# Two attentions with normalised inputs: where the norm's factor is multiplied in, and in which layout a norm is taken

## The chip, the cores and the metric

The kernel runs on one core of a Trainium2 chip. The metric is the device time of one execution in microseconds, the median of several runs. The core has five engines with a queue each: TensorE (PE in the profile; PEld is its weight load), VectorE (DVE), ScalarE (ACT), GpSimd (POOL) and SyncE (SP), which here only starts DMAs. Each executes its queue in order.

## What is computed

The reference runs two transformer blocks of two layers each, over 512 tokens (and 16 more in the first block) of width 1024. The change touches only the first layer of the second block, which has two kinds of attention on the same normalised input `hn = rms(h, g)`:

```python
aq, ak, av, bq, bk, bv = split_cols(hn @ w_in, AB_SPLITS)
# attention A, 4 heads: two softmaxes, subtracted
s  = einsum(rope(aq), rope(ak)) * 64**-0.5        # causal; two maps per head
a  = softmax(s)[0] - lam * softmax(s)[1]
ao = a @ av                                       # 128 values per head
ao = rms(ao, g_sub) * (1 - lam_init)              # norm over the 128 values
# attention B, 8 heads, dilated windows
bo = dilated_attention(rope(bq), rope(bk), bv)
y  = concat([ao, bo]) @ w_out
```

`rope(x)` is `x * cos + swap(x) * sin`, where `swap` exchanges the two halves of each head (with the sign in `sin`). Since the norm's factor, one over the root of the mean square, is a number for each token, it can be multiplied to the products of the projection instead of to `h`.

## The kernel before

Data lie transposed: features on the 128 partitions, the 512 tokens along the free dimension. Every fp32 factor is split in a high and a low part, and each product is three matmuls of a reduced fp32 type (`fp32r`): a projection of one 128-column chunk is 24 matmuls of 512 columns (8 chunks of the width, times 3) into one PSUM bank. Weights come by DMA (`wr`), ACT rounds them to `wh`, DVE or POOL takes the rest as `wl`.

The function `mixer_ab` (L1401 on) does the layer's attentions. It works in eight stages, p = 0 to 3 of A (`diff`) and then p = 0 to 3 of B (`dila`), two heads (for A, two maps of a head) in each. A stage makes `v`, then key and query by `qk`: projection, `scaled` (L1429, the PSUM bank times `rstd`, the norm's factor for each token, spread over all partitions), `rope`, and `stack`, which lays the high and low parts of each head (ACT L689, DVE or POOL L690, one DMA) into tiles that the matmuls read. `rope` (L826) is four DMAs of 32 partitions each from `v` into `sw` (L832), POOL's `v * cos` in place (L834), DVE's `sw * sin` (L835) and DVE's sum (L836). After key and query the stage transposes `v` on PE (`vt`, L1462 or L787).

`attn_pair` (L486 on) first makes scores with queries on partitions (`sm`), from which DVE takes each row's maximum (`ng`, L514); these are transposed (`ngt`) and laid into extra rows of the query (`shift_rows`, L607). Then scores with keys on partitions (`st`), ACT's exponential twice (`Ph`, `P`, L563), the low part (L564), and the products with `v` (`pv`). For A the sums of the exponentials come from a product with ones (`zs`). `diff_do` ends with `finish`: the difference of the two maps' results over their sums, its squares, a product of 128x128 ones with them that gives the sum over the 128 values on every partition (`ssq`, L1494), the mean (L1495), ACT's root (L1496), DVE's reciprocal of 128x512 in four pieces (L701), and the product (L1498). For B, `finish_pair` divides by sums that come with `pv`.

`pipeline` (L1121) sets the program's order: attention of stage p, then the making of stage p + 1, then `more`, then `finish` of stage p. The order on each engine is laid out when the kernel is built, by a planner that simulates the program and takes what is ready, earlier lines first. Buffers are rings: a new tile waits for the release of an old one. For this layer the rings are:

```python
RINGAB = dict(tmp=4, mm=2, sm=2, st=2, pv=2, ax="st")
```

`tmp` counts the 128x528 tiles in SBUF that `s.tmp(...)` hands out (`v`, `sw` and others), the rest are PSUM banks. `ax="st"` says that `vt`, `zs` and `ssq` take their banks from the ring of `st`, which has two.

Of the kernel before, what the change touches and what calls it, by code (L numbers as in the profile page):

```python
# [10 lines left out]
F32 = mybir.dt.float32  # L11
F32R = mybir.dt.float32r
BF16 = mybir.dt.bfloat16
AF = mybir.ActivationFunctionType
OP = mybir.AluOpType
# [5 lines left out]
P = 128  # L21
KC = 8
NM = 16
NX = 512
# [263 lines left out]
class Kern:  # L288
# [1112 lines left out]
    def mixer_ab(s, acts, rstd, load):  # L1401
        nc, c = s.nc, s.c
        g = Geom(0)
        tk = [(0, NX)]
        outs = [None] * 8
        with ExitStack() as sc:
            s.ap = sc.enter_context(s.tc.tile_pool(name="apab", bufs=2))
            s.yp = sc.enter_context(s.tc.tile_pool(name="ypab", bufs=2))
            kp = sc.enter_context(s.tc.tile_pool(name="kpab", bufs=1))
            s.kv_tiles(kp, NX, nq=4)  # L1410
            for i in range(4):
                s.aux_rows(i % 2, s.kt[i][0], s.qt[i][0])
            s.table("cos", 0)
            s.table("sin", 1)
            dil = s.cld("dil", kp)
            dilw = s.cld("dilw", kp, BF16)
            lv = s.tmp("lv")[:, :256].rearrange("p (a b) -> p a b", a=4)
            nc.sync.dma_start(lv, s.a["lam"])
            lam = kp.tile([P, 4], F32, name="lam")
            for i in range(2):  # L1420
                nc.vector.tensor_mul(lv[:, 2 * i], lv[:, 2 * i], lv[:, 2 * i + 1])
                nc.vector.reduce_sum(lam[:, i:i + 1], lv[:, 2 * i], axis=AX.X)
                nc.scalar.activation(lam[:, i:i + 1], lam[:, i:i + 1], AF.Exp)
            nc.vector.tensor_sub(lam[:, 2:3], lam[:, 0:1], lam[:, 1:2])
            nc.vector.tensor_scalar(lam[:, 2:3], lam[:, 2:3], LAM_INIT, -1.0, op0=OP.add, op1=OP.mult)
            o = GAIN["sub"]
            nc.vector.tensor_scalar(lam[:, 3:4], s.gain[:, o:o + 1], 1.0 - LAM_INIT, None, op0=OP.mult)

            def scaled(ch, scale=1.0):  # L1429
                v = s.tmp("v")  # L1430
                (ps, _, _), = s.proj(s.wload(s.a["wab"][ch]), acts, tk)
                nc.vector.scalar_tensor_tensor(v[:, :NX], ps, scale, rstd[:, :NX], op0=OP.mult, op1=OP.mult)  # L1432
                return v

            def keep(k, y):
                h, lo = s.t512("s", 16, F32R), s.t512("s", 16, F32R)
                s.split(y[:, :NX], h, lo)
                outs[k] = (h, lo)

            def qk(cq, ck):  # L1440
                k = scaled(ck)
                s.rope(k, 0, NX)
                heads = []
                for hn in range(2):
                    kt, qt = s.new_k(), s.new_q()
                    s.stack(k, hn, *kt, False, slice(0, NX))
                    r, d = s.MROWS[hn], s.DROW[hn]
                    if hn:
                        nc.gpsimd.memset(qt[0][d:d + 5].bitcast(F32), 0.0)
                    heads.append(dict(K1=kt[0], Q1=qt[0], QL=qt[1], lo=((kt[1], qt[1]),), drow=d, Qm=qt[0][r], Km=kt[0][r]))  # L1450
                q = scaled(cq, 0.125)
                s.rope(q, 0, NX)
                for hn in range(2):
                    s.stack(q, hn, heads[hn]["Q1"], heads[hn]["QL"], True, slice(0, NX))
                return heads

            def diff(p):
                v = scaled(8 + p)
                heads = qk(p, 4 + p)
                ps = s.bank("ax", "vt")  # L1460
                for b in range(4):
                    nc.tensor.transpose(ps[:, P * b:P * b + P], v[:, P * b:P * b + P], c["ident"])  # L1462
                vh, vl = s.vt[p % 2]
                ps = ps.rearrange("p (b f) -> p b f", b=4)
                nc.scalar.copy(vh[:, :, 0:P], ps)
                nc.vector.tensor_sub(vl[:, :, 0:P], ps, vh[:, :, 0:P].bitcast(F32))
                for hd in heads:
                    hd["V"] = lambda j: (vh[:, j, 0:P], vl[:, j, 0:P])
                return heads,

            def diff_do(p, heads):
                pv, _, zacc = s.attn_pair(g, heads, zsum=True)
                rz, o = [], []
                for m in range(2):
                    t = s.ap.tile([P, NX], F32, tag="dv", bufs=2, name=s.nm("dv"))
                    nc.scalar.copy(t, pv[m])
                    o.append(t)
                    ps = s.bank("ax", "zs")
                    nc.tensor.matmul(ps, s.ones, zacc[m], start=True, stop=True)
                    z = s.ap.tile([P, NX], F32, tag="rz", bufs=2, name=s.nm("rz"))  # L1480
                    nc.scalar.copy(z, ps)
                    rz.append(z)

                def finish():

                    y = s.yp.tile([P, NT], F32, tag="y", name=s.nm("y"))[:, :NX]
                    nc.vector.tensor_mul(y, o[0], rz[1])
                    nc.vector.scalar_tensor_tensor(o[1], o[1], lam[:, 2:3], rz[0], op0=OP.mult, op1=OP.mult)
                    nc.gpsimd.tensor_add(y, y, o[1])
                    nc.gpsimd.tensor_mul(rz[0], rz[0], rz[1])  # L1490
                    nc.scalar.activation(o[0], y, AF.Square)
                    nc.scalar.activation(rz[0], rz[0], AF.Square, scale=EPS ** 0.5)
                    ps = s.bank("ax", "ssq")
                    nc.tensor.matmul(ps, s.ones, o[0], start=True, stop=True)  # L1494
                    nc.vector.scalar_tensor_tensor(rz[0], ps, 1.0 / P, rz[0], op0=OP.mult, op1=OP.add)  # L1495
                    nc.scalar.activation(rz[0], rz[0], AF.Sqrt)  # L1496
                    s.recip(rz[0], 0, NX)
                    nc.vector.scalar_tensor_tensor(y, y, lam[:, 3:4], rz[0], op0=OP.mult, op1=OP.mult)  # L1498
                    keep(p, y)

                return finish

            smask = lambda ix, q0, k0, nk: dilw[:, k0 + 384 - q0:k0 + 384 - q0 + nk]
            tadd = lambda j, q0, n: dil[:, q0 - P * j:q0 - P * j + n]

            def dila(p):
                v = scaled(20 + p)
                heads = qk(12 + p, 16 + p)
                if p < 2:
                    s.v_ones(s.vt[p])  # L1510
                vt = s.v_pair(v, False, tail=False)[0]
                for hn, hd in enumerate(heads):
                    hd["V"] = s.vfun(vt, hn)
                return heads,

            def dila_do(p, heads):
                pv, _, _ = s.attn_pair(g, heads, smask=smask, tmask=lambda *a: None, tadd=tadd)
                yz = s.take_pair(g, pv)
                return lambda: keep(4 + p, s.finish_pair(g, *yz, None, None))

            ys = []

            def more(p):
                if p == 3:
                    s.out_part("woab", outs, 0, OUTK[0], ys, "xh", 8)
                    s.ple_load(0, lambda: s.t512("xl", 8, F32R))
                    if OUTK[1] > OUTK[0]:
                        s.out_part("woab", outs, OUTK[0], OUTK[1], ys)

            s.pipeline([(diff, diff_do, (lambda p: load()) if p == 0 else None, p) for p in range(4)] + [(dila, dila_do, more, p) for p in range(4)])  # L1530
        return s.out_part("woab", outs, OUTK[1], KC, ys)
# [233 lines left out]
```

## Time and profile before

| | us |
|---|---|
| runs | 2828.16, 2825.42, 2829.25 (median 2828.16) |
| profiled execution | 2830.3 |
| its span in the trace | 2828.5 |
| busy in the span: PE, DVE, ACT, POOL | 2708.7, 1629.7, 1225.3, 1186.1 |
| stage of the two attentions | about 1318 to 1612 |

The page gives averages over the whole span. For a change within one stage the timeline of that stage is read: which instruction an engine waits for (in brackets at the end of a line: idle time before it, and what ended it), and the busy time of each engine in each stretch.

### The profile page before, as it was taken

Reading aid. Unit: us, or ns where it says so; the run is one execution under the profiler, and the core shown is the slowest. Engines: PE = TensorE matmul, PEld = TensorE weight load, DVE = VectorE, ACT = ScalarE, POOL = GpSimd, SP = SyncE. Lnnn points to the kernel's source line nnn. Section 1 sums busy time; section 2 is a strip of 40 time slices with the busy share of each in tenths; the row PEclk is TensorE's granted clock in tenths of the full one; section 3 lists DMA queues with packets and bytes.
Section 4 is the critical chain, followed back from the end, with each engine's and each line's share of the span. In section 5 each row is a group of like instructions: output and inputs, shape, how many; then the busy total and the mean of one; then the engine's idle time right before and its main releaser. Section 6 shows DMA issues by size and latency. Waiting matters only on the chain. (4 is left out here: it accounts for less than half of the span.)

```text
span 2828.5 us, 41363 instructions
## 1 busy us (share of the span) xinstructions
PE 2708.7 (96%) x14962; PEld 2306.3 (82%) x14962; DVE 1629.7 (58%) x2997; ACT 1225.3 (43%) x2267; POOL 1186.1 (42%) x1091
## 2 busy tenths in 40 slices
PE   8999999999999999999988999999998898999998
PEld 7999999999888887877766768888776776788886
DVE  5666666644576667545688863132459876522325
ACT  4554444433454444434455543232344665322323
POOL 3455445432334334346455452133336434422333
PEclk9999999999999999999999999999999998999999
DMA  4222232234322233325322223333233212233322
GB/s 144 65 67 80 76 96 84 79 102 136 99 70 76 68 90 98 94 94 185 105 74 76 67 87 97 93 96 94 75 92 92 75 35 63 83 94 96 94 86 89
DMA packets 146669, 252.08 MB, mean 89 GB/s; under 512 B 19680, under 2 KB 32864, under 8 KB 146464
## 3 DMA queue, kind: packets, MB, share of 16 engines
q1 hardware_dynamic: 146464, 249.43, 29.5%
q8 instruction: 118, 1.93, 0.3%
q14 instruction: 87, 0.71, 0.1%
HBM read 215.26 MB, written 6.42 MB: 78 GB/s over the span
## 5 line engine op out<-in xcount | busy, mean ns | idle before, releaser
L383 ACT CAST wh<-wr 128x512 fp32r<-128x512 f32 (+3 forms) x774 | 463.8, 601 | 987.8 <-PE mm L362 815.8
L362 PE MATMUL mm<-xh,wh 128*128 128x264 f32 (+2 forms) x2464 | 849.4, 347 | 28.3 <-ACT xh L1141 8.2
L362 PE MATMUL mm<-xl,wh 128*128 128x264 f32 (+1 forms) x2480 | 852.0, 345 | 5.1 <-DVE xl L1142 1.7
L362 PE MATMUL mm<-xh,wl 128*128 128x264 f32 (+2 forms) x2464 | 845.4, 344 | 2.0 <-DVE wl L385 1.3
L385 POOL TENSOR_TENSOR wl<-wr,wh 128x512 fp32r<-128x512 f32 (+2 forms) x273 | 350.1, 1283 | 804.1 <-ACT wh L383 792.9
L385 DVE TENSOR_TENSOR wl<-wr,wh 128x512 fp32r<-128x512 f32 (+3 forms) x501 | 383.6, 766 | 398.6 <-ACT wh L383 389.9
L362 PEld LDWEIGHTS mm<-xh,wh 128*128 128x128 f32 x2464 | 469.8, 191 | 90.7 <-DVE v L1432 8.3
L362 PEld LDWEIGHTS mm<-xl,wh 128*128 128x128 f32 x2480 | 473.6, 191 | 62.2 <-DVE xl L1142 2.9
L362 PEld LDWEIGHTS mm<-xh,wl 128*128 128x128 f32 x2464 | 469.3, 191 | 58.9 <-DVE wl L385 3.2
L564 POOL TENSOR_TENSOR Pl<-P,Ph 128x512 fp32r<-128x512 f32 (+4 forms) x108 | 131.5, 1218 | 169.0 <-ACT P L563 144.9
L362 PE MATMUL mm<-fh,wl 128*128 128x512 f32 x512 | 202.3, 395 | 0.0
L362 PE MATMUL mm<-fl,wh 128*128 128x512 f32 x512 | 202.0, 395 | 0.0
L362 PE MATMUL mm<-fh,wh 128*128 128x512 f32 x512 | 202.0, 395 | 0.0
L563 ACT ACTIVATE Ph<-st 128x512 fp32r<-128x512 f32 (+4 forms) x224 | 122.1, 545 | 128.1 <-PE st L362 79.9
L564 DVE TENSOR_TENSOR Pl<-P,Ph 128x512 fp32r<-128x512 f32 (+4 forms) x108 | 83.1, 769 | 123.6 <-ACT P L563 110.7
L362 PE MATMUL mm<-c,wh 128*128 128x264 f32 (+2 forms) x480 | 127.9, 353 | 9.5 <-ACT q L1645 4.7
L1320 POOL TENSOR_TENSOR ff<-ff 128x512 f32<-128x512 f32 x64 | 82.2, 1286 | 106.3 <-DVE ff L1319 106.3
L701 DVE RECIPROCAL zr<-zr 128x128 f32<-128x128 f32 (+1 forms) x144 | 123.2, 916 | 2.7 <-ACT zr L710 2.4
L563 ACT ACTIVATE P<-st 128x512 f32<-128x512 f32 (+4 forms) x216 | 116.8, 541 | 6.5 <-POOL Pl L564 3.0
L483 POOL TENSOR_TENSOR acc<-acc,sq 128x512 f32<-128x512 f32 (+1 forms) x64 | 92.0, 1442 | 60.6 <-ACT sq L479 54.8
L362 PEld LDWEIGHTS mm<-fl,wh 128*128 128x128 f32 x512 | 96.5, 188 | 22.5
L362 PEld LDWEIGHTS mm<-fh,wl 128*128 128x128 f32 x512 | 96.5, 188 | 22.3
(612 smaller groups left out, 5154.2 us busy)
## 6 DMA issues: line engine op xcount, KB each, us to landing
wr<-in_win_dram SPq DMA_DIRECT2D x240, 256.0 KB
wr<-in_wmi_dram SPq DMA_DIRECT2D x128, 256.0 KB
wr<-in_wmo_dram SPq DMA_DIRECT2D x128, 256.0 KB
wr<-in_wbr_dram SPq DMA_DIRECT2D x48, 256.0 KB
wr<-in_wab_dram SPq DMA_DIRECT2D x48, 256.0 KB
wr<-in_wout_dram SPq DMA_DIRECT2D x32, 256.0 KB
wr<-in_wpg_dram SPq DMA_DIRECT2D x32, 256.0 KB
wr<-in_wuq_dram SPq DMA_DIRECT2D x32, 192.0 KB
```

Of the source, the lines that this page charges most:

```text
L362: s.nc.tensor.matmul(out, l, r, start=start, stop=stop)
L383: nc.scalar.copy(h, raw)
L385: s.weng[s.wn % len(s.weng)].tensor_sub(l, raw, h.bitcast(F32))
L483: e[eng[1]].tensor_add(sums.t[:, :T], sums.t[:, :T], q[:, :T])
L563: nc.scalar.activation(o[:, :col], ps[:, :col], AF.Exp)
L564: s.pl_eng(ui, hn).tensor_sub(pl[:, :col], p[:, :col], ph[:, :col].bitcast(F32))
L701: s.nc.vector.reciprocal(t[:, a:b], t[:, a:b])
L1320: nc.gpsimd.tensor_mul(f, f, f)
```

## The change

The norm's factor goes into the two rope tables once, ahead of all stages: `cos` and `sin` are multiplied by `rstd` and by 64 to the power -1/4, so that key and query carry the square root of the scores' scale each. A new function `roped` takes the place of `scaled` and `rope` for keys and queries. ACT copies the PSUM bank to a new tile `raw` of the ring tmp; DVE multiplies the same bank with the table `cos` into `v`; the four DMAs go from `raw` into `sw`; POOL multiplies `sw` with `sin`; DVE adds. `scaled` stays for `v`, as a plain product.

In `finish` of A the sum over the 128 values is taken with tokens on partitions. `col_sums` makes, for each block of 128 tokens, a matmul with that block as the stationary operand and a column of ones as the moving one: four of the squares and four of the small term that stands for epsilon, into four columns of one bank. ACT's root and DVE's reciprocal are then of 128x4 elements. Four matmuls with the identity, whose stationary operand is a column of the result read 128 times over, bring it back along the tokens on every partition, into a second bank (`rb`) of the ring of `st`, which the last product reads.

```diff
-            def scaled(ch, scale=1.0):
+            def scaled(ch):
...
-                nc.vector.scalar_tensor_tensor(v[:, :NX], ps, scale, rstd[:, :NX], op0=OP.mult, op1=OP.mult)
+                nc.vector.tensor_mul(v[:, :NX], ps, rstd[:, :NX])
...
+            for n in ("cos", "sin"):
+                nc.vector.scalar_tensor_tensor(c[n][:, :NX], c[n][:, :NX], 64.0 ** -0.25, rstd[:, :NX],
+                                               op0=OP.mult, op1=OP.mult)
+
+            def roped(ch):
+                v, raw, sw = s.tmp("v"), s.tmp("raw"), s.tmp("sw")
+                (ps, _, _), = s.proj(s.wload(s.a["wab"][ch]), acts, tk)
+                nc.scalar.copy(raw[:, :NX], ps)
+                nc.vector.tensor_mul(v[:, :NX], ps, c["cos"][:, :NX])
+                for b in range(4):
+                    d = 32 * (b ^ 1)
+                    nc.sync.dma_start(sw[32 * b:32 * b + 32, :NX], raw[d:d + 32, :NX])
+                nc.gpsimd.tensor_mul(sw[:, :NX], sw[:, :NX], c["sin"][:, :NX])
+                nc.vector.tensor_add(v[:, :NX], v[:, :NX], sw[:, :NX])
+                return v
+
             def qk(cq, ck):
-                k = scaled(ck)
-                s.rope(k, 0, NX)
+                k = roped(ck)
...
-                q = scaled(cq, 0.125)
-                s.rope(q, 0, NX)
+                q = roped(cq)
...
                     ps = s.bank("ax", "ssq")
-                    nc.tensor.matmul(ps, s.ones, o[0], start=True, stop=True)
-                    nc.vector.scalar_tensor_tensor(rz[0], ps, 1.0 / P, rz[0], op0=OP.mult, op1=OP.add)
-                    nc.scalar.activation(rz[0], rz[0], AF.Sqrt)
-                    s.recip(rz[0], 0, NX)
-                    nc.vector.scalar_tensor_tensor(y, y, lam[:, 3:4], rz[0], op0=OP.mult, op1=OP.mult)
+                    s.col_sums(ps, o[0], NX, True, False)
+                    s.col_sums(ps, rz[0], NX, False, True)
+                    r = s.tp.tile([P, 8], F32, tag="rc", bufs=4, name=s.nm("rd"))
+                    nc.scalar.activation(r[:, :4], ps[:, :4], AF.Sqrt, scale=1.0 / P)
+                    nc.vector.reciprocal(r[:, :4], r[:, :4])
+                    ps = s.bank("ax", "rb")
+                    for b in range(4):
+                        nc.tensor.matmul(ps[:, P * b:P * b + P], r[:, b:b + 1].to_broadcast([P, P]), c["ident"],
+                                         start=b == 0, stop=b == 3)
+                    nc.vector.scalar_tensor_tensor(y, y, lam[:, 3:4], ps, op0=OP.mult, op1=OP.mult)
```

## Rows read from the trace of the kernel before

**Rows 1.** The page: busy time, share of span, instructions of each engine.

```profile
PE 2708.7 (96%) x14962; PEld 2306.3 (82%) x14962; DVE 1629.7 (58%) x2997; ACT 1225.3 (43%) x2267; POOL 1186.1 (42%) x1091
```

**Rows 2.** Stretches: length, busy PE, PEld, DVE, ACT, POOL (instructions); granted clock, DMA.

```profile
1397.00:1430.30 33.30, 31.50 (x140) 24.08 (x139) 27.82 (x45) 18.74 (x33) 19.77 (x16) 0.92 0.25 73
...
1430.30:1466.30 36.00, 30.69 (x141) 23.62 (x140) 29.45 (x47) 18.95 (x33) 19.99 (x16) 0.95 0.27 75
1466.30:1501.20 34.90, 29.95 (x142) 22.41 (x141) 28.92 (x46) 18.75 (x34) 21.14 (x18) 1.00 0.27 78
1501.20:1531.40 30.20, 26.06 (x119) 20.39 (x117) 26.58 (x48) 16.41 (x28) 16.22 (x13) 1.00 0.26 75
...
1564.10:1587.30 23.20, 23.20 (x120) 19.85 (x120) 21.00 (x44) 15.75 (x32) 11.84 (x10) 1.00 0.36 105
...
1451.00:1453.00 2.00, 2.00 (x6) 1.52 (x6) 2.00 (x4) 1.99 (x5) 0.31 (x1) 0.50 0.20 48
```

**Rows 3.** Waits of PE, 1315 to 1610: total us, times, longest.

```profile
PE mm L362 <- DVE v L1432: 5.9, 6, 1.5
PE st L362 <- DVE rz L1495: 4.9, 3, 2.8
...
PE sm L362 <- DVE ng L514: 2.7, 3, 1.4
PE ngt L362 <- DVE ng L514: 1.5, 2, 1.2
```

**Rows 4.** Timelines of DVE, SP and POOL: start, length, engine, line, operation.

```profile
1400.85 1.38 DVE L836 TENSOR_TENSOR v<-v,sw 128x512 f32<-128x512 f32 x1
1402.27 0.69 DVE L1432 SCALAR_TENSOR_TENSOR v<-mm,rstd 128x512 f32<-128x512 f32 x1
...
1427.80 0.69 DVE L690 TENSOR_TENSOR k3l<-v,k3h 64x512 fp32r<-64x512 f32 x1
...
1428.56 2.46 SPq L832 DMA_DIRECT2D sw<-v  x4
...
1432.67 1.46 POOL L834 TENSOR_TENSOR v<-v,cos 128x512 f32<-128x512 f32 x1 [3.60 <-DMA sw<-v]
```

**Rows 5.** Timeline of PE, 1430 to 1449.

```profile
1430.32 0.60 PE L1462 MATMUL vt<-c_ident,v 128*128 128x128 f32 x4
...
1432.37 0.50 PE L362 MATMUL mm<-xh,wh 128*128 128x512 f32 x1 [1.46 <-DVE v L1432]
...
1448.84 0.50 PE L362 MATMUL st<-q1l,k1l 128*128 128x512 f32 x1 [2.79 <-DVE rz L1495]
```

**Rows 6.** The rope's lines and a copy from PSUM: ns minimum/median/maximum, or busy us, mean ns.

```profile
L1432 DVE SCALAR_TENSOR_TENSOR v<-mm,rstd x24: 670/684/692, 1325.6 to 1556.0; 128x512 f32<-128x512 f32 x24
...
L835 DVE TENSOR_TENSOR sw<-sw,sin x16: 678/694/1790, 1334.2 to 1563.0; 128x512 f32<-128x512 f32 x16
...
L835 DVE TENSOR_TENSOR sw<-sw,sin 128x512 f32<-128x512 f32 x16 | 16.6, 1038 | 14.0 <-DMA sw<-v 13.5 <-issue 0.5
...
L1284 ACT COPY xh<-mm 128x512 f32<-128x512 f32 x8 | 4.7, 588 | 0.0
```

**Rows 7.** The norm's lines, and the same work in other layouts near 1310 and 1324.

```profile
L701 DVE RECIPROCAL rz<-rz 128x128 f32<-128x128 f32 x16 | 13.5, 901 | 1.0 <-ACT rz L1496 1.0
...
L1495 DVE SCALAR_TENSOR_TENSOR rz<-ssq,rz 128x512 f32<-128x512 f32 x4 | 2.7, 677 | 0.0
...
1309.21 1.84 PE L418 MATMUL ssq<-ones,acc 128*128 128x1 f32 x16
...
1323.90 1.88 PE L453 MATMUL rb<-rstd,ones 128*128 128x512 f32 x4
...
L438 DVE RECIPROCAL rc<-rc x2: 177/178/178, 1318.7 to 1319.8; 128x4 f32<-128x4 f32 x2
```

**Rows 8.** The last stage's query cast on ACT, and its maxima on PE.

```profile
1568.52 0.63 ACT L689 CAST q2h<-v 64x512 fp32r<-64x512 f32 x1
...
1587.64 0.31 PE L362 MATMUL ngt<-c_identr,ng 128*128 128x128 f32 x1
```

## Prediction

> **What bounds the kernel now.** The page first: TensorE (PE) is busy for 96% of the span, VectorE (DVE) for 58% [rows 1]. An average over 2828 us says little of a change that lives in one stage, so next the timeline of the stage of the two attentions (about 1318 to 1612 us), cut at the points where its pipeline turns over. A turn begins, at a time that I call T, when the transposes of `v` for pair p run on PE: at 1396.9, 1430.3, 1466.4, 1501.2, 1531.4, 1564.1 and 1587.3 us. In the four turns from 1397 to 1531 PE is busy for 31.50, 30.69, 29.95 and 26.06 us of 33.30, 36.00, 34.90 and 30.20, and DVE for 27.82, 29.45, 28.92 and 26.58 [rows 2]. So PE is the bound with some 16 us of idle time in four turns (the differences summed), and DVE is close behind. Third, what PE waits for in the stage: the product `v` of L1432 (5.9 us), the `ssq` bank's release by `rz` L1495 (4.9), the row maxima `ng` (2.7 and 1.5) [rows 3].
>
> Why PE waits for L1432 is the point to see. DVE is not late with it: it has no place to write. All of `v`, the rotated keys and queries, and their swapped copies `sw` come from one ring of four buffers (tag tmp, `RINGAB`). The add of L836 that frees one `sw` ends at 1400.85 + 1.38 = 1402.23, and the next L1432 starts at 1402.27; the last reader of a key, k3l at 1427.80 + 0.69 = 1428.49, and the next four DMAs into `sw` go out at 1428.56 [rows 4]. I compared all sixteen first writes into the ring between 1392 and 1499 with the buffer releases in front of them (those two are the pattern): eleven follow one within 0.1 us, the rest within 0.8. The ring is full, and is handed out in the order of the program. At T the transposes end (1430.32 + 0.60), the buffer of the old `v` goes to a waiting product, and PE gets its PSUM bank back (two banks, mm) and resumes at 1432.37, that is T + 2.05 [rows 5].
>
> The second ring that binds is st, two PSUM banks, which also serves `vt`, `zs` and `ssq`. The second head's scores wait 2.79 us for `ssq` at 1448.84 [rows 5].
>
> **The change part by part.**
>
> **Rope.** Per rope (16 of them) DVE's product with the sine (L835, 1038 ns mean, 16.6 us) goes to GpSimd (POOL) in place of its product with the cosine, which DVE does straight from PSUM in place of the scaling L1432 (684 ns) [rows 6]. POOL's count stays, and its product had to wait for the same DMAs before, because it overwrote what they read. ScalarE (ACT) gains 16 copies from PSUM; the nearest row is the copy `xh` from mm, 588 ns: 9.4 us [rows 6]. L1432 (one operand from PSUM) always takes 670 to 692 ns, and L835 678 at its best but up to 1790, so I take 684 ns for the new product [rows 6]. [...]
>
> The copy and the product read the same bank. No row shows two engines reading one bank independently, so the bank may be held for 0 to 0.59 us longer per rope; between these I take 0 for PE, since the buffer wait below is longer. [...] At 16 x 0.59 that is 9.4 us of bank time, behind waits that are longer.
>
> **The ring.** Each rope now needs three buffers at once (`v`, `raw`, `sw`) instead of two, and the ring still has four. Follow the order. Before T the old `v` of pair p holds one buffer, `v` of pair p+1 the second, `raw` and `v` of key p+1 the third and fourth: full. The DMAs into that key's `sw` cannot go until the transposes free the first, at T. In the kernel before, that key was long done at T, and its query's DMAs were out (1428.56, T - 1.8). Now from T on: transposes 0.60, DMAs go at T + 0.7, POOL starts 4.11 later (1428.56 to 1432.67) and takes 1.46, the add 1.38 [rows 4, 5]: `sw` is free at T + 7.6, and only then is there a buffer for the query's product, 0.68 more. PE gets the bank at about T + 8.3 instead of T + 2.05. In the four turns from 1397 to 1531 it has nothing else: the other bank holds the next `v`, which is behind in the ring, and the scores of the next attention come behind `ssq` in st. That is 6.3 us idle for each. Against it, projections left over from there fill the present waits for the second head (2.79 and, twice, less: 4.9 in all [rows 3, 5]), 1.2 per turn. 4 x (6.3 - 1.2) = **+20.4 us**. Ends: 8 (the scores start some 3 us earlier, since the bank no longer waits for L1495) and 32. In the three later turns scores or output matmuls stand ready, and I count nothing for them here.
>
> [...]
>
> **The difference's norm** (four times). Away: one fp32 product `ssq`; at the pace of `rb`, the same shape twice in 1.88 us, 0.9 us of PE. Away on DVE: L1495 (0.68 each) and four times four reciprocals of 901 ns (13.5 us in all) [rows 7]. Added on PE: eight column sums; sixteen such instructions took 1.84 us. Four broadcasts of 128 columns: no row; the four fp32 transposes took 0.60, the bound below, and the 1.88 of `rb`, a longer product twice, the bound above; 0.9, since the columns are those of `ssq`. On DVE a 128x4 reciprocal, 178 ns; on ACT a root of 128x4 instead of 128x512, a gain left at nothing [rows 5, 7]. PE gains 1.84 + 0.9 - 0.9 = 1.84, four times 7.4 us. Half of it lies in the new idle: **+3.7** (0 to 11). It also takes two banks of st in turn instead of one, root and reciprocal between them; who waits for that is the next attention's scores. The first bank is free after the root and no longer after L1495, so I set these against each other at nothing.
>
> **DVE's relief.** Away 16.6 + 13.5 + 2.7 = 32.8 us, added two table products (0.7 to 1.0 each) and 0.7 us of reciprocals: some 30 us of the 113 that DVE is busy in four turns and of what follows. On the path that is worth the waits that DVE itself causes, the row maxima: **-4.2** [rows 3]. The two table products stand ahead of the first `v`: +0.7 (0 to 1.5).
>
> **The last pair.** Its query's casts come at 1568.52, 4.4 us behind T = 1564.1, and its maxima reach PE (`ngt`) at 1587.64 [rows 8]. By the chain above the key's DMAs now go at T + 0.7, and the query's after the key's casts, some 10 us later again: casts at about T + 19. The row maxima have slack, output matmuls keep PE busy for all of 1564.1 to 1587.3 [rows 2], and then little does: **+4** (0 to 10).
>
> Sum: 20.4 + 2.7 + 3.7 - 4.2 + 0.7 + 4 = 27.3 us. The profiled execution took 2830.3 (span 2828.5), 2.1 above the median: 2857.6 by its own time, 2855 beside the median.
>
> **The rivals.** *DVE's relief decides (faster).* Place: the waits of PE in these turns. If the planner hands the ring out so that the key's `sw` is written before T (the point from which it decides), the ropes are done as early as now. Then relief could remove the 15 us of rows 3 and the clock lost in two turns (0.08 x 33 + 0.05 x 36 = 4.5), against 7.4 of PE work and 2 for tables and banks: -10 us, 2818. For it: DVE is busy for over 80% of the turns; against it: sixteen hand-overs in program order. *The pieces cancel.* The ring costs PE little because row maxima and scores are brought forward: half of the 7.4 of PE work against the relief's 4.2: 2828. *Only the banks cost.* The ring does no harm, but `ssq` and the broadcast take st one after the other, behind a busy ACT: four times 2 us, and 7.4 of PE, less 4.2: +11, 2839.
>
> **How the numbers follow.** Ring 0.56 (2855, its own range 2836 to 2878), only the banks 0.12 (2839), cancel 0.10 (2828), relief 0.22 (2818). A measurement of this kernel tells 0.2%, 5.7 us, from no change. Faster 0.22, same 0.10, slower 0.68. The range is 2819 to 2878: it leaves out about half of the relief case and what lies above 32 us of ring with all other ends dear.
>
> **What would show it.** Right: the first DMAs into `sw` of a key go within 0.2 us behind the transposes of the `v` before; PE's gap behind the transposes grows from 2 us to over 6; the turns up to 1531 lengthen by 4 to 7 us each; DVE's busy time falls by some 30 us and gives nothing back. Wrong: keys rotated before T, or turns that shorten; then the relief was worth more than the ring. If instead the gap stands before the next scores, and not behind the transposes, it was the banks.

## The result, and the profile after

The changed kernel takes 2844.95 us (median of 2838.87 to 2849.66), the kernel before 2827.2 beside it: ratio 1.0061, 95% interval 1.0047 to 1.0075, **17.7 us slower**. The forecast was 27 us slower (2855); the range held the time and the sign was right. The profiled execution is the slowest of its four (2849.66, span 2847.9).

The page after, engines (busy time, share, instructions), to be read against [rows 1]:

```profile
PE 2721.2 (96%) x15050; PEld 2321.3 (82%) x15050; DVE 1591.3 (56%) x2967; ACT 1234.8 (43%) x2283; POOL 1178.9 (41%) x1091
```

DVE has lost 38.4 us of work, and the kernel is slower. The turns of the changed kernel begin (T) at 1386.88, 1427.07, 1464.87, 1502.68, 1538.73, 1562.24 and 1599.94 us. The stretches between them, with the columns of [rows 2]:

```profile
1386.90:1427.10 40.20, 35.21 (x164) 28.38 (x163) 22.22 (x39) 20.21 (x36) 18.68 (x16) 0.87 0.23 65
1427.10:1464.90 37.80, 33.59 (x163) 27.55 (x162) 20.31 (x41) 19.86 (x35) 18.83 (x16) 0.91 0.22 64
1464.90:1502.70 37.80, 33.35 (x163) 27.35 (x162) 20.93 (x41) 19.86 (x35) 19.75 (x19) 0.91 0.26 71
1502.70:1538.70 36.00, 31.55 (x145) 27.00 (x144) 21.75 (x42) 17.84 (x32) 15.22 (x15) 0.86 0.26 74
```

The four turns are 6.8, 1.8, 3.0 and 5.8 us longer than before; DVE is now busy for 54 to 60% of them instead of over 80%; the granted clock was between 0.92 and 1.00 and is between 0.86 and 0.91. Timeline of PE in the second of them (start, length, engine, line, operation; in brackets the idle time before it and what ended it), the counterpart of [rows 5]:

```profile
1427.07 0.60 PE L1477 MATMUL vt<-c_ident,v 128*128 128x128 f32 x4
1427.43 0.31 PE L362 MATMUL ngt<-c_identr,ng 128*128 128x128 f32 x1
1431.95 1.87 PE L418 MATMUL ssq<-ones,dv 128*128 128x1 f32 x8 [4.21 <-ACT dv L1506]
1433.68 1.85 PE L418 MATMUL ssq<-ones,rz 128*128 128x1 f32 x8
1435.38 0.77 PE L362 MATMUL mm<-xh,wh 128*128 128x512 f32 x1
...
1441.65 1.05 PE L1517 MATMUL rb<-c_ident,rd 128*128 128x128 f32 x8
1442.46 0.47 PE L362 MATMUL st<-q0l,k0l 128*128 128x512 f32 x1
```

And the other engines in the same stretch (SP, ACT, POOL, DVE), the counterpart of [rows 4]:

```profile
1427.70 2.45 SPq L1452 DMA_DIRECT2D sw<-raw  x4
...
1431.80 0.57 ACT L1448 COPY raw<-mm 128x512 f32<-128x512 f32 x1
...
1431.84 1.26 POOL L1453 TENSOR_TENSOR sw<-sw,sin 128x512 f32<-128x512 f32 x1 [0.60 <-DMA sw<-raw]
...
1433.13 0.69 DVE L1454 TENSOR_TENSOR v<-v,sw 128x512 f32<-128x512 f32 x1 [2.52 <-POOL sw L1453]
1433.93 0.69 DVE L1449 TENSOR_TENSOR v<-mm,cos 128x512 f32<-128x512 f32 x1
```

This is the chain of the prediction, link by link. The transposes of the old `v` end at 1427.67; the four DMAs of the next key go at 1427.70; POOL starts at 1431.84 (T + 4.8) and ends at 1433.10; the add ends at 1433.82, and with the buffer that it frees the query's product L1449 starts at 1433.93. It ends at 1434.62, T + 7.6, and the bank is free, somewhat ahead of the forecast T + 8.3: POOL's product and the add took 1.26 and 0.69 us, for 1.46 and 1.38 in the forecast. PE is back at projections at 1435.38, which is T + 8.3 too, but that is luck. What was not forecast is that PE does something in between: at 1431.95 the squares of the difference are ready, and the norm's column sums run for 3.4 us, until the projections take over without a gap. In the four turns PE is back at projections at T + 8.3 to T + 9.1, each time straight behind the column sums. PE's waits in the stage (1315 to 1610), with the columns of [rows 3]:

```profile
PE ssq L418 <- ACT dv L1506: 17.9, 4, 4.8
PE pv L362 <- ACT Ph L563: 7.0, 4, 4.3
PE mm L362 <- DVE v L1432: 1.8, 1, 1.8
...
PE sm L362 <- DVE ng L514: 0.4, 1, 0.4
```

One gap of 4.2 to 4.8 us behind each of four sets of transposes (17.9 in all) has taken the place of many small ones: the waits for L1432 fell from 5.9 to 1.8, those for the `ssq` bank from 4.9 to nothing, those for the row maxima from 4.2 to 0.4 [rows 3]. The likely reason, which no run here isolates, is that the others catch up while PE stands still.

For a sum that doesn't hang on where a turn is cut, I take the whole stage, from the first column sum ahead of it (L418) to the end of the last add of its output (L1287). Within it all kernels with the old norm have 1285 PE instructions in the records, those with the new one 1373 (e11, below, 1341). Before and after:

```profile
1309.21:1625.30 316.09, 286.09 (x1285) 221.32 (x1283) 254.87 (x431) 160.76 (x296) 163.89 (x147) 0.96 0.31 91
```

```profile
1306.78:1639.13 332.35, 298.99 (x1373) 240.68 (x1371) 215.49 (x402) 168.73 (x312) 153.14 (x147) 0.92 0.30 86
```

The stage is 16.3 us longer: PE's idle time grew from 30.0 to 33.4 and its busy time from 286.1 to 299.0. The spans differ by 19.4: the stage begins 2.4 us earlier, and 5.5 us come behind it, in a stage that was not changed and whose order was laid out anew; I did not follow those.

### The profile page after: what moved, and what is told of

Its sections match the earlier page's. It is cut to its first block, busy times and chain, and to the rows that moved or that the text cites. A ratio compares the mean times of both kernels' runs of the same rounds, so it can differ in the third digit from the quotient of the medians.

```text
span 2847.9 us, 41558 instructions
## 1 busy us (share of the span) xinstructions
PE 2721.2 (96%) x15050; PEld 2321.3 (82%) x15050; DVE 1591.3 (56%) x2967; ACT 1234.8 (43%) x2283; POOL 1178.9 (41%) x1091
## 4 chain that ended last, share of the span: by engine, by line
PE 83%; DVE 10%; ACT 3%; issue 2%; POOL 1%; DMA 1%; SPq 0%; DVEq 0%; POOLq 0%; ACTq 0%
PE mm L362 69%; PE st L362 5%; PE pv L362 5%; PE ssq L418 1%; PE sm L362 1%; DVE zr L701 1%; DVE h L1273 1%; DVE sc L1732 1%; DVE m L1731 1%; DVE sm L514 1%; DVE s L1270 1%; DVE wl L385 1%; DVE xl L1248 1%; DVE Pl L564 0%; PE rb L453 0%
## 5 line engine op out<-in xcount | busy, mean ns | idle before, releaser
L362 PE MATMUL mm<-c,wh 128*128 128x264 f32 (+2 forms) x480 | 128.6, 355 | 10.1 <-ACT q L1666 4.8
L362 PEld LDWEIGHTS mm<-fh,wh 128*128 128x128 f32 x512 | 96.5, 188 | 22.4
```

The lines of the kernel that those rows point to most:

```text
L362: s.nc.tensor.matmul(out, l, r, start=start, stop=stop)
```

## Experiments

The same view of that stage gives one line for each kernel; idle is the length less PE's busy time, for each kernel from one profiled execution. Each ratio is to runs of the kernel before that were taken beside it (medians 2827.2 to 2828.5 us). "Ring" is `RINGAB`'s tmp.

| kernel | ring | median us | ratio (95%) | stage | PE busy | PE idle | clock |
|---|---|---|---|---|---|---|---|
| before | 4 | 2827.2 | 1 | 316.1 | 286.1 | 30.0 | 0.96 |
| after | 4 | 2844.95 | 1.0061 (1.0047, 1.0075) | 332.4 | 299.0 | 33.4 | 0.92 |
| e1 new rope alone | 4 | 2845.53 | 1.0058 (1.0040, 1.0075) | 332.9 | 291.9 | 41.0 | 0.92 |
| e2 new norm alone | 4 | 2827.66 | 0.9997 (0.9986, 1.0008) | 317.0 | 289.5 | 27.5 | 0.98 |
| e3 after | 5 | 2823.5 | 0.9980 (0.9968, 0.9991) | 309.0 | 289.0 | 20.0 | 0.97 |
| e4 before | 5 | 2832.38 | 1.0016 (1.0004, 1.0029) | 321.6 | 291.6 | 30.0 | 0.96 |
| e5 before | 3 | 2853.31 | 1.0088 (1.0075, 1.0101) | 338.8 | 292.4 | 46.4 | 0.93 |
| e6 rope with two buffers, new norm | 4 | 2826.7 | 0.9999 (0.9988, 1.0010) | 316.0 | 291.0 | 25.0 | 0.98 |
| e7 new rope alone | 5 | 2816.02 | 0.9955 (0.9941, 0.9968) | 306.8 | 283.8 | 23.0 | 0.96 |
| e8 rope with two buffers, new norm | 5 | 2829.22 | 1.0000 (0.9990, 1.0011) | 321.9 | 297.5 | 24.4 | 0.96 |
| e9 after, `v` made last | 4 | 2828.59 | 0.9997 (0.9986, 1.0009) | 318.5 | 292.1 | 26.4 | 0.96 |
| e10 new rope alone, `v` last | 4 | 2826.44 | 0.9994 (0.9980, 1.0007) | 314.4 | 286.7 | 27.7 | 0.95 |
| e11 after, one set of sums | 5 | 2837.6 | 1.0034 (1.0022, 1.0047) | 322.7 | 292.6 | 30.1 | 0.95 |
| e12 new rope alone, `v` last | 5 | 2813.35 | 0.9935 (0.9916, 0.9955) | 305.2 | 281.5 | 23.7 | 0.97 |

### Which half of the change: e1 and e2

e1 takes `roped`, the scaled tables and the plain product for `v`, and leaves `finish` as before; e2 does the reverse.

> The change's rope (tables scaled once, raw copy, product from PSUM) with the norm of the kernel before. Ring theory (the third buffer of each rope finds no place in the ring of four, so a key's swap DMAs wait for the transposes of the value before): nearly the whole loss of the change stays, +10 to +18 us against before (2837 to 2845), with the DMAs into sw right behind the transposes. Bank theory (the norm's two banks of the st ring hold up the next scores): no loss here, -5 to +3 us. Relief theory (DVE's work was what held PE): faster, -5 us or more.

> The change's norm (column sums, 128x4 root and reciprocal, broadcast into a second bank) with the rope of the kernel before. Ring theory: small, -4 to +6 us (7.4 us more PE work, part of it in idle time, against the waits for the release of ssq, 4.9 us, and DVE's reciprocals). Bank theory: +8 to +16 us, nearly the whole loss.

The stage's line of e1:

```profile
1307.68:1640.60 332.92, 291.92 (x1285) 227.02 (x1283) 237.52 (x418) 170.81 (x312) 153.71 (x148) 0.92 0.30 86
```

The rope alone makes the whole loss (1.0058), the norm alone none (0.9997). In e1 the key's DMAs go 0.63 us after T, with the end of the transposes, in all six turns. The instructions of PE are those of before, 1285: idle time is 11.0 us more, and busy time 5.8 us more, at a lower clock (whether the clock makes it is taken up further below). The new norm, put on top (after against e1), adds 7.1 us of busy time and takes 7.6 of idle time away, so that in sum it costs nothing there: its column sums lie in the gap. In e2, which has no such gap, it costs nothing either (3.4 us more busy, 2.5 less idle). That the two `st` banks carry the loss is refuted by e1 and e2.

### The ring by its size: e3, e4, e5

```diff
-RINGAB = dict(tmp=4, mm=2, sm=2, st=2, pv=2, ax="st")
+RINGAB = dict(tmp=5, mm=2, sm=2, st=2, pv=2, ax="st")
```

in the changed kernel (e3) and in the kernel before (e4); `tmp=3` in the kernel before (e5).

> The changed kernel with five buffers in the ring tmp instead of four, nothing else. Ring theory: a key's swap no longer waits for the transposes, PE's gap behind the transposes falls from 4.2-4.8 us to about 2 us or less, and most of the loss goes: 2825 to 2834. Bank theory: within 4 us of the changed kernel, 2841 to 2849.

> The kernel before with five buffers in the ring tmp instead of four, nothing else. Ring theory: the ring was full there too and PE waited for it behind each transpose (1.45 us, four times) and at half clock: -3 to -10 us (2817 to 2824). If the ring did not bind before: within 3 us.

> The kernel before with a ring of three buffers instead of four, nothing else. Ring theory (what costs is that the key's swap DMAs find no free buffer until the old v is transposed): with three, old v, next v and the key's product fill the ring, so the key's DMAs go right behind the transposes, as in the changed kernel, though nothing of the change is in it. Expect +15 to +35 us against the kernel before (2843 to 2863) and the first DMAs of a key within 1 us behind the transposes of every turn up to 1531. Rival (the loss comes from the new rope's own operations: the copy on ACT, two readers of one bank, POOL's turn in the chain): within 6 us of the kernel before.

With a fifth buffer the changed kernel is 21 us faster and passes the kernel before. (Another ring also means another order of the whole stage; e4 shows 4 us from that.) Timeline of e3, PE and then SP:

```profile
1425.41 0.60 PE L1477 MATMUL vt<-c_ident,v 128*128 128x128 f32 x4
1426.79 0.50 PE L362 MATMUL mm<-xh,wh 128*128 128x512 f32 x1 [0.79 <-DVE v L1432]
...
1422.41 2.44 SPq L1452 DMA_DIRECT2D sw<-raw  x4
```

The key's DMAs go 3.0 us ahead of T (2.0 to 3.1 in the four turns), and PE waits 0.79 us behind the transposes and is then at projections. So the loss goes with the wait for that buffer. e5 makes the same wait in the kernel before, with nothing of the change in it: with three buffers, old `v`, next `v` and key fill the ring. Timeline of e5, PE's transposes and SP's DMAs in two turns:

```profile
1422.76 0.60 PE L1462 MATMUL vt<-c_ident,v 128*128 128x128 f32 x4
...
1423.39 2.45 SPq L832 DMA_DIRECT2D sw<-v  x4
...
1462.04 0.60 PE L1462 MATMUL vt<-c_ident,v 128*128 128x128 f32 x4
...
1462.67 2.45 SPq L832 DMA_DIRECT2D sw<-v  x4
```

In all six turns from 1388 to 1565 they go 0.63 to 0.65 us after T, within 0.05 us of the transposes' end, and the kernel loses 25 us (16.4 of them idle time of PE in the stage). The idle time is not one gap here: behind three of the first four transposes PE has scores or projections to do, and it stands still later, most of all for the row maxima (12.5 us against 4.2). The late key costs, but where PE stands still for it depends on what else is ready.

e4 was a miss. I read the waits for L1432 in the kernel before as a ring that is full, which it is; but a fifth buffer makes that kernel no faster, rather 4 us slower, with the same 30.0 us of idle time: the waits for `Pl` (7.0 us), for the row maxima (7.3) and for L1432 itself (6.8) stand where others stood. Nor were the waits behind the transposes what I wrote, four times 1.45 us and at half clock: they are 0.78, 1.46, 1.45 and 1.45 us, the last two in turns at a granted clock of 1.00 [rows 2]. A resource that is always full is not for that reason worth time. The gaps of the changed kernel were for want of a buffer (21 us came back with one more); those of the kernel before, though they lay behind the same ring, were not.

### The ring by its order and by the rope's need: e6, e8, e9

e6 (ring of four) and e8 (ring of five) need two buffers for a rope:

```diff
-                v, raw, sw = s.tmp("v"), s.tmp("raw"), s.tmp("sw")
+                v, sw = s.tmp("v"), s.tmp("sw")
...
-                nc.scalar.copy(raw[:, :NX], ps)
-                nc.vector.tensor_mul(v[:, :NX], ps, c["cos"][:, :NX])
+                nc.scalar.copy(v[:, :NX], ps)
...
-                    nc.sync.dma_start(sw[32 * b:32 * b + 32, :NX], raw[d:d + 32, :NX])
+                    nc.sync.dma_start(sw[32 * b:32 * b + 32, :NX], v[d:d + 32, :NX])
+                nc.vector.tensor_mul(v[:, :NX], v[:, :NX], c["cos"][:, :NX])
```

e9 leaves the change as it is and makes `v` last in a stage:

```diff
-                v = scaled(8 + p)
                 heads = qk(p, 4 + p)
+                v = scaled(8 + p)
```

(and the same in `dila`).

> The changed kernel with a rope that needs two buffers instead of three, ring of four: ACT copies the bank to v, the DMAs go from v, DVE multiplies v with the scaled cosine in place (after the DMAs, no more from PSUM). Scaled tables, POOL's product with the sine, ACT's copy and the new norm stay. Ring theory: the third buffer alone was the loss, so 2820 to 2832, key DMAs ahead of the transposes, PE's gap behind them under 2 us. Rival (ACT's copy or POOL in the chain costs): the loss stays, 2840 to 2850.

> The rope with two buffers and the new norm, ring of five. Two theories on where the 9 us between the whole change at five buffers (2823.5) and the kernel before at five (2832.4) come from. The product read straight from PSUM, without waiting for DMAs, carries it: this one lies near the kernel before at five, 2828 to 2834. Scaled tables and the lighter norm carry it: near the whole change at five, 2820 to 2827.

> The whole change, ring of four, with one difference: a stage makes key and query first and v last (two lines change places in each kind of attention), so the ring is handed out in another order. Ring theory: it is the order that made the key wait: v of the next pair no longer holds a buffer while its key and query are turned, so the key's three buffers fit beside the old v. Expect the key's swap DMAs ahead of the transposes in the turns up to 1531, PE's gap behind them under 2.5 us, and 2816 to 2832. Rival (the number of buffers is what counts, whoever holds them): the loss stays, 2840 to 2850.

Each takes the loss away with four buffers: e6 is level with before (0.9999), and so is e9 (0.9997), which changes only who asks for buffers first. Timeline of e9, SP and PE:

```profile
1452.40 2.44 SPq L1452 DMA_DIRECT2D sw<-raw  x4
...
1455.31 0.60 PE L1477 MATMUL vt<-c_ident,v 128*128 128x128 f32 x4
1456.69 0.50 PE L362 MATMUL mm<-xh,wh 128*128 128x512 f32 x1 [0.78 <-DVE v L1432]
```

The key's DMAs go 2.9 us ahead of the transposes again, and the gap is 0.78 us. ACT's copy and POOL's place in the rope's chain are in e6 too, so they cost no more than the rest of the change gains. e8 is level with before too: a fifth buffer gives nothing to a rope that needs two (e4, e8). It gives 21 us or more to the one that needs three (e3 against after, e7 against e1). At five buffers e8 and e3 differ only in the rope: the cosine product of e3 reads PSUM and need not wait until the DMAs have read `v`, and e3 is 5.7 us faster (their two intervals overlap by a hair).

### What the norm is worth where the ring is free: e7, e10, e11, e12

e7 is e1 with `tmp=5`, e10 is e1 with `v` last, e12 has both. e11 is e3 with POOL adding the small term to the squares, and one `col_sums`:

```diff
+                    nc.gpsimd.tensor_add(o[0], o[0], rz[0])
...
-                    s.col_sums(ps, o[0], NX, True, False)
-                    s.col_sums(ps, rz[0], NX, False, True)
+                    s.col_sums(ps, o[0], NX, True, True)
```

> The new rope with the norm of before and a ring of five. Ring theory: the new rope is free of its loss at five buffers, so 2820 to 2828. Compared with the whole change at five (2823.5) it tells what the new norm is worth there: within 3 us of it if the norm is off the path, 4 to 8 us slower if it is the relief of DVE by the norm (16 us of reciprocals and means) that carries the gain at five.

> The rope alone with the norm of before, ring of four, v made last. By the ring theory 2814 to 2828. Beside the whole change with v last it tells what the new norm is worth where the ring doesn't bind: with rings of five the norm cost 7.5 us (2823.5 against 2816.0), which is close to its extra PE work (7.4 us by the rows of before). If that is so, this one is 4 to 9 us faster than the whole change with v last; if the 7.5 was a matter of that one order, the two lie within 3 us.

> The whole change with a ring of five, and one set of column sums in the norm instead of two: POOL adds the small term to the squares first, so eight matmuls of one column (four for two passes each) fall away in each of the four stages of A. If the norm's 7.5 us at five buffers are PE's extra work, half of the column sums' time goes, 3 to 4 us: 2818 to 2821.5. If they are the wait between sums and broadcast (root, reciprocal and two banks), nothing is gained, and POOL's addition lengthens it: 2822 to 2828.

> The rope alone, v last and a ring of five: the two ways of freeing the ring together. If each only takes the same wait away, the two together are worth no more than one: 2811 to 2822, as the rope alone at five (2816.0). If buffers are still short with five, 2800 to 2811.

e7 is 7.5 us faster than e3, faster than I had expected of it: with the ring free, the new norm is a cost (the two intervals just touch). With `v` last and four buffers (e10 against e9) it is 2.2 us, within the intervals; by what was expected of e10 that speaks for a matter of one order and against PE's added work. e12 is the fastest, 0.9935 of the kernel before, no further from e7 (2.7 us) than the intervals allow.

e11 answered neither way: eight PE instructions fewer in each of four stages, and 14 us slower than e3. Timeline of PE in one turn, e3 and then e11 (there with DVE's reciprocal):

```profile
1436.40 0.95 PE L418 MATMUL ssq<-ones,dv 128*128 128x1 f32 x8
1437.21 1.03 PE L418 MATMUL ssq<-ones,rz 128*128 128x1 f32 x8
...
1440.63 1.07 PE L1517 MATMUL rb<-c_ident,rd 128*128 128x128 f32 x8
1441.46 0.47 PE L362 MATMUL st<-q0l,k0l 128*128 128x512 f32 x1
```

```profile
1444.61 0.95 PE L418 MATMUL ssq<-ones,dv 128*128 128x1 f32 x8
...
1449.31 0.17 DVE L1514 RECIPROCAL rd<-rd 128x4 f32<-128x4 f32 x1
1449.45 0.79 PE L362 MATMUL mm<-xh,wh 128*128 128x512 f32 x1 [3.44 <-DVE v L1449]
...
1455.28 1.05 PE L1517 MATMUL rb<-c_ident,rd 128*128 128x128 f32 x8
1456.09 0.48 PE L362 MATMUL st<-q0l,k0l 128*128 128x512 f32 x1
```

T is 1425.41 in e3 and 1430.95 in e11. From T the sums come at 11.0 and 13.7 us, the broadcast at 15.2 and 24.3, the next attention's first scores at 16.1 and 25.1. In e11 the root and the reciprocal are done by 1449.48 (1449.31 + 0.17), but in PE's queue the broadcast stands behind a projection that waits 3.44 us for its bank, and the scores stand behind the broadcast. So two matmuls with a root between them are a place at which a queue in order can put 6 us of other work (here 1449.48 to 1455.28). This is one turn; I did not add up the 14 us. Whether the 7.5 us between e7 and e3 are of that kind or PE's added work stays open: their profiled executions (2818.0 and 2818.7) lie too close together to show it.

## Why the prediction was right, by its steps

**What bounds the kernel, and the ring.** The mechanism is shown: the key's DMAs go 0.03 to 0.21 us behind the transposes in the six turns from 1387 to 1562, the query's bank is free at T + 7.6 to T + 8.2 in the first four, and the loss goes with a fifth buffer (e3), with a rope of two (e6) or with another order (e9), and comes without the change when a buffer is taken away (e5). The time alone would not have shown it: 2845 lies nearer to the rival of the banks (2839) than to the forecast (2855), and it is e1 and e2 that tell the two apart. Of the signs that I named, the DMAs and DVE's time came as forecast, the gap is 4.2 to 4.8 us and not over 6, and of the four turns two are longer by 4 to 7 us (6.8 and 5.8) and two by less (1.8 and 3.0).

**Its size was too large.** I took 4 x (6.3 - 1.2) = 20.4 us of idle time, on the premise that PE "has nothing else" between T and T + 8.3. That premise failed: the gap was 4.2 to 4.8 us, since the column sums came into it, and in e1 PE had scores and 15 or 16 projection matmuls to do behind two of the four sets of transposes. And the 1.2 per turn of present waits that it would absorb was too small: the small waits of PE that vanished (L1432 4.1, the `ssq` bank 4.9, the row maxima 3.8, POOL's `zacc` 3.4) come to 16.2 us, some 4 per turn. By my terms idle time in the stage was to grow by about 17 (20.4 + 4 for the last pair + 0.7, less 4.2 of relief and 3.7 for norm work laid into it); it grew by 3.4, and by 11.0 in e1.

**The clock's term.** The 2.7 us of the sum was my allowance for a lower clock, an estimate: one turn of 33 us at 0.92 in place of 1.00 [rows 2]. No run shows this term; what the runs showed in its place is the granted clock itself. In the whole change the four turns' granted clock fell by 0.05, 0.04, 0.09 and 0.14 [rows 2], which times their lengths is 12.0 us, an estimate from these rows, part of it idle. So the clock fell by more than I allowed; what that cost is not shown. In e1 the same 1285 instructions are busy for 5.8 us longer at 0.92 in place of 0.96, but in e4 they are busy for 5.5 us longer than before at an equal 0.96:

```profile
1304.06:1625.67 321.61, 291.58 (x1285) 221.81 (x1283) 259.21 (x431) 160.17 (x296) 163.35 (x147) 0.96 0.31 89
```

In the kernel before, the clock of a turn does not go with the idle time in it: the turn from 1397, at 0.92, has the least idle time of the four, 1.80 us (33.30 - 31.50), and the two turns at 1.00 have 4.95 and 4.14 [rows 2]. Its clock was low before it began:

```profile
1392.50:1396.90 4.40, 3.30 (x7) 1.50 (x6) 2.75 (x5) 1.66 (x3) 0.99 (x2) 0.50 0.42 114
```

In the changed kernel the fall of the clock is plain. Behind the gap of 4.21 us the granted clock is 0.50:

```profile
1432.00:1438.00 6.00, 6.00 (x22) 5.51 (x23) 2.78 (x4) 3.06 (x5) 2.37 (x2) 0.50 0.24 55
```

that is under the column sums and the first projections; in the stretch from 1439.5 to 1441.5 it is 1.00. PE busy time was to grow by 2.7 + 7.4 = 10.1 and grew by 12.9. The two errors, about 14 us too much idle time and 3 too little busy time, are the 11 between the forecast (27.3) and the stage (16.3); they have opposite signs, so the sum came nearer than its main term.

**The norm.** Its extra work on PE was about 7.4 us by the forecast; it is 7.1 between e1 and the changed kernel, and 3.4 to 5.4 between the other pairs that differ in the norm alone (before and e2, e7 and e3, e10 and e9). The +3.7 that I put on the path should have been nothing with four buffers (e2: 0.9997, no difference within the interval). The bank rival falls with it as the cause of the loss. The times that I had taken from other rows: broadcast 1.05 us for 0.9; sixteen column sums 1.84 us at a granted clock of 1.00 in e3 (from 1436.40 to 1437.21 + 1.03), as forecast, and 3.58 at 0.50 in the changed kernel (from 1431.95 to 1433.68 + 1.85).

**The rope's instructions.** L1448 was taken from `xh` at 588 ns, L1449 from L1432 at 684. Durations of after (minimum, median, maximum in ns):

```profile
L1448 ACT COPY raw<-mm x16: 567/581/594, 1323.0 to 1566.9; 128x512 f32<-128x512 f32 x16
L1449 DVE TENSOR_TENSOR v<-mm,cos x16: 677/684/692, 1325.0 to 1572.4; 128x512 f32<-128x512 f32 x16
...
L1454 DVE TENSOR_TENSOR v<-v,sw x16: 677/693/1768, 1332.9 to 1579.3; 128x512 f32<-128x512 f32 x16
```

The add, with both operands in SBUF, is no shorter at its best (677 ns) than the product that reads PSUM (677). What two readers of one bank cost was not put to the test: in the changed kernel the product starts 0.1 to 4.9 us after the end of the copy of the same bank in all sixteen ropes.

**DVE's relief.** Some 30 us were to go and give nothing back. They went (38.4 by the page) and gave nothing back with four buffers. I priced them at 4.2 on the path, and the rival case, where the keys are turned before T, at 10 us faster in all. With five buffers that case is there: e7 is 12 us faster than the kernel before, e3 5 (and e4 says that the buffer itself gives none of it). No run gains without turning the key before T, and that alone is not enough: e9 and e10 do that with four buffers and are level with before.

**The last pair.** Key's DMAs at T + 0.7 and query's casts at about T + 19 were forecast; T is 1562.24:

```profile
1562.91 2.44 SPq L1452 DMA_DIRECT2D sw<-raw  x4
1574.00 2.45 SPq L1452 DMA_DIRECT2D sw<-raw  x4
...
1580.22 0.62 ACT L689 CAST q2h<-v 64x512 fp32r<-64x512 f32 x1
```

They came at T + 0.67 and T + 18.0. The last two turns together are 5.4 us longer (23.5 and 37.7 against 32.7 and 23.2), but PE is busy for 37.13 us of the last 37.70: that is no idle time, work has moved there from elsewhere. The idle time that I had in mind was to come behind the last T, when the output matmuls are done. From there to the end of the stage, before and after:

```profile
1587.29:1625.30 38.01, 32.85 (x135) 23.87 (x134) 30.67 (x50) 21.30 (x47) 12.75 (x14) 0.91 0.12 34
...
1599.94:1639.13 39.19, 31.93 (x136) 23.95 (x134) 30.31 (x55) 20.58 (x45) 11.93 (x13) 0.91 0.11 32
```

PE is idle for 5.2 us of it before and for 7.3 after, 2.1 more for a forecast of 4; the largest wait is 4.28 us for `Ph`, at 1608.16. In e1 it is idle for 10.4 us there, 6.38 of them in one wait for `s` (L408): of the 11.0 us of idle time that e1 adds, 5.2 lie in this tail and not behind the transposes. That the late query makes these waits I did not follow. The part ahead of the first T is 7.6 us shorter, which I had not foreseen at all. With an order that is laid out anew, work crosses the borders of turns, and only the whole stage can be summed.

## What to carry to other kernels

Count how many buffers of a ring a step holds at once, and write down in program order who holds them when the ring is full: one more per step cost 17 us here, and a fifth buffer, or asking for `v` last, took it back. A ring that is always full may still cost nothing, so try its size in both directions before reading its waits as time. When a wait is added, take off all smaller waits that will vanish into it, not only those next to it, and let the work that is ready by then run in it; what remains of it can be paid a second time: here the granted clock was 0.50 for some 6 us behind a gap of 4.21 us, and the sixteen column sums in them took 3.58 us in place of the 1.84 of e3 at 1.00.

## What the runs showed of the chip

The clock's effect on a single kind of instruction is plain: the eight instructions of one set of column sums took 0.95 us at a granted clock of 1.00 (e3) and 1.87 us at 0.50 (the changed kernel, behind its gap of 4.21 us). Its effect on the whole stage is not, and that was new to me: PE's busy time is no constant of the work and the clock. The same 1285 PE instructions were busy for 283.78 us in e7, 286.09 before and 291.58 in e4, each at a mean granted clock of 0.96; on PE they differ in the order of the work. So the 291.92 of e1 at 0.92 can't be read as the price of the clock.
